# A decoder layer on one core: each modulation tile loaded and summed in one step, its sum queued behind the low part traced last

## The chip, the core and the metric

The kernel runs on one core of one Trainium2 chip. The metric is device time in microseconds (us) of one execution, and the median of several runs is compared. A profile is one execution recorded by the hardware profiler; its span goes from the first to the last instruction. The engines are TensorE (PE in the profile, its weight loads PEld), VectorE (DVE), ScalarE (ACT), GpSimd (POOL) and SyncE (SP), whose queue issues most transfers.

## The reference

One decoder layer over 256 tokens of width 2048, all in float32. A vector `c` gives six modulation vectors (shift, scale and gate for each of two sub-layers):

```python
mod = jax.nn.silu(c) @ w_ada[l] + b_ada[l]
sh1, sc1, g1, sh2, sc2, g2 = jnp.split(mod[:, None, :], 6, axis=-1)
h = x * (1.0 + sc1) + sh1
y = token_mixer(h, w_in[l], conv_w[l], a_log[l], dt_bias[l], gdn_norm_w[l], rel_bias,
                w_proj_moba[l], w_proj_gdn[l], w_out[l])
x = layer_norm(DEEPNORM_ALPHA * x + g1 * y, ln1_g[l], ln1_b[l])
h = x * (1.0 + sc2) + sh2
y = swiglu(h, w_ffn_in[l], w_ffn_out[l])
x = layer_norm(DEEPNORM_ALPHA * x + g2 * y, ln2_g[l], ln2_b[l])
```

The token mixer projects h to the inputs of a softmax attention (MoBA; with 256 tokens only its own causal block counts) and of a gated delta rule, runs both, projects and merges their outputs by sigmoid gates, and projects the sum. The modulation alone is a product of a 2048-vector with a 2048 x 12288 matrix: 100 MB that are read once and used for one multiplication per element.

## The kernel before

**Weights.** Every weight matrix is streamed in tiles of 128 partitions x 1024 float32 (0.5 MB). `step` lists one tile's work: `load_w` issues the transfer into `raw` on SP, `split_w` makes the rounded high part `hi` on ScalarE (L221) and the low part `lo = raw - hi` on VectorE (L222), and the matmuls take hi and lo three times over (L306 to L308 for 256 columns of tokens, L313 and L317 or L354 to L356 in the other layouts). One tile is 24 matmuls of 256 columns or their equal. `raw` is a ring of six buffers, `hi` and `lo` are rings of four each. `run(3)` writes the program down so that the loads and splits of up to four tiles ahead are traced before the matmuls of the current one.

**Modulation tiles.** The 12288 x 2048 matrix is laid out by output column, so that the product is a sum along the free axis: VectorE multiplies a tile by the broadcast silu(c) `cb` and adds up in one instruction (`ada_sum`, L241), and a short second instruction reads the accumulator. The first 40 columns come in the opening, in whole rows (tile `r`). The other 56 columns come later in two halves each, 112 tiles `raw_a` of 0.5 MB, which take their buffers from the same ring of six as the weights (L251). `ada_sums` is a generator: each advance issues one transfer and one sum. With its argument `ahead` at 1, the first advance issues two transfers, and every sum then belongs to the tile issued one advance earlier. Before each generator of 8 columns ends, its last tile is summed without a new load. The sum of the first half goes into `ada_half`, that of the second into `adac`.

**Pace.** `tick()` is called after the matmuls of every tile. It advances the lane "ada" 0.32 times a tick in the first part of the mixer, 0.85 times from the merge on, and 0.2 times in the second network; and it advances the background lanes with the small work of the two mixers: the convolutions (L581), the decay matrices (L685 to L701), the recursion that inverts the triangular blocks on VectorE (Mb, Ub, tm, L723 to L731), the block products (L754 to L818), the output norm (yb, L868) and the attention (L906 to L940).

**Order.** The kernel is written in a layer that schedules: instructions are taken by priority (in the main, the order in which they were traced) as soon as the layer's own timing model has their inputs ready. On each engine the resulting order is fixed, and the engine goes through it in that order; it waits at an instruction whose input is missing, and everything behind it waits too. `keep_in_program_order(i)` ties instruction i behind the one traced just before it on the same engine. It adds no wait on the chip, only an order. In the kernel before it is used for one low part of the second network, for some of the norm's operations and for a table load.

Of the kernel before, what the change touches and what calls it, by code (L numbers as in the profile page):

```python
# [13 lines left out]
OP = mybir.AluOpType  # L14
# [7 lines left out]
KT = D // P  # L22
# [71 lines left out]
def layer(ctx, tc, a, out):  # L94
    nc = tc.nc
    v_, s_, g_, t_, dma = nc.vector, nc.scalar, nc.gpsimd, nc.tensor, nc.sync
# [21 lines left out]
    cols = perm.tile([P, V_END], F32, name="cols")  # L118
# [8 lines left out]
    cb = perm.tile([P, D], F32, name="cb")  # L127
# [25 lines left out]
    adac = perm.tile([P, 96], F32, name="adac")  # L153
    w_ada = a["w_ada"]

    bg = {"moba": [], "main": [], "pre": [], "ada": []}
# [77 lines left out]

    ada_half = perm.tile([P, 64], F32, name="ada_half")

    def ada_sum(col, part, raw, parts):
        first, last = part == 0, part == parts - 1
        n = D // parts
        h = ada_half[:, col % 4:col % 4 + 1]  # L240
        v_.tensor_tensor_reduce(out=raw, in0=raw, in1=cb[:, n * part:n * part + n], scale=1.0,  # L241
                                scalar=cols[:, col:col + 1] if first else h, op0=OP.mult, op1=OP.add,
                                accum_out=adac[:, col:col + 1] if last else h)

    def ada_sums(order, ahead):
        todo = [(col, half) for col in order for half in range(2)]
        held = []
        for n in range(len(todo) + ahead):
            if n < len(todo):
                col, half = todo[n]  # L250
                raw = wp.tile([P, 1024], F32, tag="raw", name="raw_a", bufs=6)  # L251
                dma.dma_start(raw, w_ada.tile(8 * half, 8, col * P, P, by_column=True))
                held.append((col, half, raw))
            if n >= ahead:
                ada_sum(*held.pop(0), 2)
                yield 1.35

    def ada_opening(order, ahead, at_once, between):
# [61 lines left out]
    def pairs_of(ps):  # L320
        return ps.rearrange("p (t i) -> p t i", t=2)
# [91 lines left out]
    ada_order = [v * KT + j for k0, kn in GROUPS for j in range(k0, k0 + kn) for v in range(2)]  # L413
    ada_order += [v * KT + j for v in (2, 4, 3) for j in range(KT)]
    EARLY = 8
# [32 lines left out]
    def add_ba():  # L448
        wbs = [k1.tile([P, KT, 32], F32R, tag="c2", name=x, bufs=4) for x in ("wbh", "wbl")]
        split(*wbs, wba)  # L450
        ps = pg.tile([P, 512], F32, tag="gd", name="ps_ba")
        for f in range(KT):
            for w, h in ((0, 0), (0, 1), (1, 0)):
                t_.matmul(ps[:32, :S], wbs[w][:, f, :], h_ops[h][f], start=(f == 0 and w + h == 0),
                          stop=(f == KT - 1 and w == 1))
        s_.copy(ba, ps[:32, :S])
# [376 lines left out]
    def gdn_pre(b):  # L833
        yield from conv(kqs[b][:, 0:4, :], 4 * b)
        yield from conv(kqs[b][:, 4:8, :], 8 + 4 * b)
        yield from conv(vts[b], 16 + 8 * b)
        if b == 0:
            yield from until("begun")
            yield from zero_dram()
            make_sel()  # L840
        yield from gdn_qk(b)
        done.add(f"k{b}")
        yield from until("gates")
        yield from gdn_v(b)
        done.add(f"v{b}")
        pass

    def gdn_norm(b):
        yield from until(f"c{b}")
        o = bvs[b]  # L850
        on = c2("on", [P, 4, 2, 8])
        ss = on[:, 0]
        for h in range(8):
            for i in range(2):
                sq = c2("osq", [P, P])
                s_.activation(sq, o[:, i, h, :], AF.Square, accum_out=ss[:, i, h:h + 1])
            if h % 2 == 1:
                yield rest()
        v_.tensor_scalar(ss, ss, 1.0 / HD, None, op0=OP.mult)
        rs = on[:, 1]  # L860
        rsqrt(rs, on[:, 2], on[:, 3], ss, epsc[:, 0:1])
        yield 0.6
        yield from until(f"z{b}")
        yb = ybs[b]
        for h in range(8):
            for i in range(2):
                ys = yb[:, i, h * HD:(h + 1) * HD]
                v_.scalar_tensor_tensor(ys, o[:, i, h, :], rs[:, i, h:h + 1], ys, op0=OP.mult, op1=OP.mult)  # L868
            if h % 2 == 1:
                yield 1.1  # L870
        done.add(f"n{b}")

    def gdn_turn(b):
        yield from until(f"n{b}")
        yield rest()
        yb = ybs[b]
        if b == 0:
            hl = k1.tile([P, 2, 8, S], F32R, tag="ma0", name="ybA")
            hi, lo = hl[:, 0], [hl[:, 1, 0:4], hl[:, 1, 4:8]]
        else:  # L880
            hi = k1.tile([P, 8, S], F32R, tag="ma1", name="ybBh")
            lo = [k1.tile([P, 4, S], F32R, tag="m4", name="ybBl", bufs=3) for _ in range(2)]
        for f in range(8):
            ybT[0].append(hi[:, f, :])
            ybT[1].append(lo[f // 4][:, f % 4, :])
        for f in range(0, 8, 2):
            tp = pt.tile([P, 2, S], F32, tag="tp", name="tp")
            for i in range(2):
                for h in range(2):
                    t_.transpose(tp[:, i, h * P:(h + 1) * P], yb[:, h, (f + i) * P:(f + i + 1) * P], ident)  # L890
            split(hi[:, f:f + 2, :], lo[f // 4][:, f % 4:f % 4 + 2, :], tp, nwc)
            yield 0.6
            if f == 2:
                yield rest()
        done.add(f"t{b}")
# [49 lines left out]
    def begin():  # L945
        turn["all"] = True
        add_ba()
        ya = perm.tile([P, 2, MH, S], F32R, tag="s2", name="ya")
        for x in range(2):
            ya_ops[x].extend(ya[:, x, k, :] for k in range(MH))  # L950
        done.add("begun")
        pace.update(all=2.0, ada=0.32)
        bg["pre"] += [gdn_pre(1), gdn_norm(0)]
        bg["main"] += [gates_ba(), gdn_chain(0), gdn_chain(1), gdn_turn(0), gdn_norm(1), gdn_turn(1)]
        bg["moba"] += [moba(2), moba(3), moba(0), moba(1)]
        bg["ada"] += [ada_sums(ada_order[n:n + 8], 1) for n in range(2 * KT + EARLY, len(ada_order), 8)]

    do(begin)
    cur = {}

# [232 lines left out]
    def act(j, psg, psu):  # L1193
        ach, acl = cur["act"]
        sg = k3_tile("sg")
        s_.activation(sg, psg, AF.Silu)
        v_.tensor_tensor(sg, psu, sg, op=OP.mult)
        split(ach[:, 2 * j:2 * j + 2, :], acl[:, 2 * j:2 * j + 2, :], sg)
# [31 lines left out]
    begun, held = len(prog), []  # L1230
# [28 lines left out]
    def ffn_more():  # L1259
        act(0, pairs_of(pss[0]), pairs_of(pss[1]))  # L1260
        act(1, pairs_of(pss[2]), pairs_of(pss[3]))
        bg["main"].append(ln1_affine())
        bg["ada"].append(ada_sums(range(5 * KT, 6 * KT), 1))
        pace["ada"] = 0.2

    do(ffn_more)

    def ffn_unit(j):
# [115 lines left out]
```

## Time and profile before

| | us |
|---|---|
| median of 3 runs | 1711.68 |
| lowest and highest run | 1706.76 and 1713.21 |
| span of the profiled execution | 1708.3 |
| its TensorE busy | 1651.7 |
| its VectorE busy | 1235.5 |
| its ScalarE busy | 838.7 |

The profiled execution has no time of its own beside its span: the span is what the profiler gives, and the median of the runs lies 3.4 us above it. In the lines of the profile, an entry such as `[4.90 <-DVE lo L222]` says that the engine stood idle for 4.90 us before this instruction and that VectorE's `lo` at line 222 ended this. In the tables of waits the numbers are the total in us, how often, and the longest. In the tables of stretches each engine has its busy time and, in brackets, its instructions; the last three columns are the granted TensorE clock, the mean busy share of the 16 DMA engines, and GB/s. Line numbers are those of the kernel before; in the changed kernel everything from L245 on stands two lines lower.

### The profile page before, as it was taken

The numbers are of one execution on the slowest core, as the hardware profiler recorded it, in microseconds if no ns is written. First come the engines' busy times: TensorE is split into PE (matmuls) and PEld (weight loads), VectorE is DVE, ScalarE is ACT, GpSimd is POOL, SyncE is SP. The second block draws the span as 40 slices with busy tenths as digits, with TensorE's granted clock in tenths as the row PEclk, the third lists the DMA queues.
The fourth block names the chain that finished last, engine by engine and source line by source line (L and its number), as shares of the span: only waits on it lengthen the run. The fifth ranks groups of instructions, "written<-read, shape, count | busy, mean of one in ns | idle before, by whom it ended". The sixth has DMA issues, their size and how long they took to land.

```text
span 1708.3 us, 28200 instructions
## 1 busy us (share of the span) xinstructions
PE 1651.7 (97%) x11077; PEld 1482.3 (87%) x11077; DVE 1235.5 (72%) x1768; ACT 838.7 (49%) x1199; POOL 34.6 (2%) x60
## 2 busy tenths in 40 slices
PE   5899999999999998999999999999999999999997
PEld 4899999888999798889988998888888888888885
DVE  6899999787985676557989786666666666455454
ACT  3544445579653763364434454444444444433341
POOL 0000000010010000000000000000000000000000
PEclk9999999999999999999999999999999999999998
DMA  9999996666775577557899477777777776665661
GB/s 369 338 355 343 352 338 217 202 195 199 237 260 186 172 229 244 189 187 242 312 358 362 150 226 256 231 227 232 231 227 231 236 230 221 234 192 189 200 191 72
DMA packets 113750, 412.72 MB, mean 242 GB/s; under 512 B 13405, under 2 KB 14445, under 8 KB 108109
## 3 DMA queue, kind: packets, MB, share of 16 engines
q1 hardware_dynamic: 110178, 400.13, 69.4%
q0 software_dynamic: 3440, 10.80, 2.4%
q8 instruction: 87, 1.43, 0.3%
q14 instruction: 45, 0.37, 0.1%
HBM read 406.59 MB, written 4.28 MB: 241 GB/s over the span
## 4 chain that ended last, share of the span: by engine, by line
PE 61%; DVE 8%; DMA 5%; issue 2%; ACT 1%; DVEq 0%; ACTq 0%
PE mm L313 17%; PE mm L317 9%; PE mm L354 7%; PE mm L355 7%; PE mm L356 7%; DMA raw_a<-in_w_ada 4%; DVE lo L222 3%; PE mm L306 3%; PE mm L307 3%; PE mm L308 3%; DVE raw_a L241 1%; DMA Mb<-mbd 1%; PE ps L754 1%; DMA raw<-in_w_out 0%; ACT hi L221 0%
## 5 line engine op out<-in xcount | busy, mean ns | idle before, releaser
L221 ACT CAST hi<-raw 128x1024 fp32r<-128x1024 f32 (+2 forms) x576 | 582.6, 1015 | 706.2 <-PE mm L356 197.1
L222 DVE TENSOR_TENSOR lo<-raw,hi 128x1024 fp32r<-128x1024 f32 (+2 forms) x576 | 673.5, 1177 | 295.8 <-ACT hi L221 293.4
L306 PE MATMUL mm<-s,hi 128*128 128x256 f32 x1232 | 350.7, 285 | 15.9 <-ACT s L229 12.0
L308 PE MATMUL mm<-s,lo 128*128 128x256 f32 x1232 | 348.0, 283 | 13.1 <-DVE lo L222 12.9
L307 PE MATMUL mm<-s,hi 128*128 128x256 f32 x1232 | 346.8, 282 | 0.0
L313 PE MATMUL mm<-s,hi 128*128 128x512 f32 x1280 | 319.5, 392 | 0.0
L313 PEld LDWEIGHTS mm<-s,hi 128*128 128x128 f32 x1280 | 228.5, 188 | 39.4
L306 PEld LDWEIGHTS mm<-s,hi 128*128 128x128 f32 x1232 | 234.3, 190 | 21.0 <-ACT s L229 13.6
L308 PEld LDWEIGHTS mm<-s,lo 128*128 128x128 f32 x1232 | 235.8, 192 | 15.7 <-DVE lo L222 15.5
L307 PEld LDWEIGHTS mm<-s,hi 128*128 128x128 f32 x1232 | 234.8, 191 | 1.5 <-issue 1.1
L317 PEld LDWEIGHTS mm<-s,lo 128*128 128x128 f32 x1280 | 169.9, 188 | 13.6
L317 PE MATMUL mm<-s,lo 128*128 128x256 f32 x1280 | 171.9, 277 | 0.0
L354 PE MATMUL mm<-hi,ach 128*128 128x512 f32 x352 | 137.0, 389 | 0.0
L356 PE MATMUL mm<-hi,acl 128*128 128x512 f32 x352 | 136.9, 389 | 0.0
L355 PE MATMUL mm<-lo,ach 128*128 128x512 f32 x352 | 136.9, 389 | 0.0
L241 DVE CUSTOM_DVE_ANT_0 raw_a<-raw_a,cb,ada_half 128x1024 f32<-128x1024 f32 x56 | 71.7, 1280 | 53.3 <-DMA raw_a<-in_w_ada 53.3
L241 DVE CUSTOM_DVE_ANT_0 raw_a<-raw_a,cb,cols 128x1024 f32<-128x1024 f32 x56 | 71.8, 1281 | 51.1 <-DMA raw_a<-in_w_ada 51.0
L241 DVE CUSTOM_DVE_ANT_0 r<-r,cb,cols 128x2048 f32<-128x2048 f32 x40 | 93.4, 2346 | 9.4 <-ACT cb L137 9.4
L354 PE MATMUL mm<-hi,s 128*128 128x512 f32 x192 | 78.7, 410 | 0.0
L355 PEld LDWEIGHTS mm<-lo,ach 128*128 128x128 f32 x352 | 66.1, 188 | 13.8
L354 PEld LDWEIGHTS mm<-hi,ach 128*128 128x128 f32 x352 | 66.1, 188 | 13.8
L356 PEld LDWEIGHTS mm<-hi,acl 128*128 128x128 f32 x352 | 66.1, 188 | 13.6
(314 smaller groups left out, 2265.6 us busy)
## 6 DMA issues: line engine op xcount, KB each, us to landing
raw<-in_w_ffn_in SPq DMA_DIRECT2D x176, 512.0 KB, 4.3
raw<-in_w_in SPq DMA_DIRECT2D x160, 512.0 KB, 4.3
raw_a<-in_w_ada SPq DMA_DIRECT2D x112, 512.0 KB, 4.5
raw<-in_w_ffn_out SPq DMA_DIRECT2D x88, 512.0 KB, 4.2
r<-in_w_ada SPq DMA_DIRECT2D x40, 1024.0 KB, 8.0
raw<-in_w_in SPq DMA_DIRECT2D x48, 384.0 KB, 5.7
raw<-in_w_proj_gdn SPq DMA_DIRECT2D x32, 512.0 KB, 4.6
raw<-in_w_out SPq DMA_DIRECT2D x32, 512.0 KB, 5.9
```

The costliest lines, as they stand in the source:

```text
L221: s_.copy(hi, raw)
L222: low = v_.tensor_tensor(lo, raw, hi.bitcast(F32), op=OP.subtract)
L241: v_.tensor_tensor_reduce(out=raw, in0=raw, in1=cb[:, n * part:n * part + n], scale=1.0, scalar=cols[:, col:col + 1] if first else h, op0= ...
L306: t_.matmul(o, hi[:, i, c], ah, start=(first and i == 0 and t == 0), stop=False)
L307: t_.matmul(o, hi[:, i, c], al, start=False, stop=False)
L308: t_.matmul(o, lo[:, i, c], ah, start=False, stop=(last and i == kn - 1 and t == 1))
L313: t_.matmul(box[t].rearrange("p (u i) -> p u i", u=2), hi[:, i, t * P:(t + 1) * P], both[k0 + i], start=(first and i == 0), stop=False)
L317: t_.matmul(box[t][:, :S], lo[:, i, t * P:(t + 1) * P], both[k0 + i][:, 0, :], start=False, stop=(last and i == kn - 1))
L354: t_.matmul(box[h], xh, hi[:, i, :], start=start, stop=False)
L355: t_.matmul(box[h], xh, lo[:, i, :], start=False, stop=False)
L356: t_.matmul(box[h], xl, hi[:, i, :], start=False, stop=stop)
L754: t_.matmul(ps[to, n, :], lhs(n), rhs(n), start=True, stop=True)
```

## The change

Two things change, and both concern only the 112 tiles `raw_a`. `ahead` is 0 in all generators of `ada_sums`, so each advance issues a transfer and, in the same breath, the sum of that same tile. And the sum is tied behind the VectorE instruction traced last before it. Since the tiles of `run(3)` are traced ahead, this is in most cases the `lo` of a weight tile that will be used three or four tiles later. The opening (`ada_opening`) calls `ada_sum` without the tie and is as it was. The number of tiles, their bytes, the sums and the pace are the same.

```diff
-    def ada_sum(col, part, raw, parts):
+    def ada_sum(col, part, raw, parts, pin=False):
         first, last = part == 0, part == parts - 1
         n = D // parts
         h = ada_half[:, col % 4:col % 4 + 1]
-        v_.tensor_tensor_reduce(out=raw, in0=raw, in1=cb[:, n * part:n * part + n], scale=1.0,
-                                scalar=cols[:, col:col + 1] if first else h, op0=OP.mult, op1=OP.add,
-                                accum_out=adac[:, col:col + 1] if last else h)
+        added = v_.tensor_tensor_reduce(out=raw, in0=raw, in1=cb[:, n * part:n * part + n], scale=1.0,
+                                        scalar=cols[:, col:col + 1] if first else h, op0=OP.mult, op1=OP.add,
+                                        accum_out=adac[:, col:col + 1] if last else h)
+        if pin:
+            tc.keep_in_program_order(added)
...
             if n >= ahead:
-                ada_sum(*held.pop(0), 2)
+                ada_sum(*held.pop(0), 2, True)
                 yield 1.35
...
-        bg["ada"] += [ada_sums(ada_order[n:n + 8], 1) for n in range(2 * KT + EARLY, len(ada_order), 8)]
+        bg["ada"] += [ada_sums(ada_order[n:n + 8], 0) for n in range(2 * KT + EARLY, len(ada_order), 8)]
...
-        bg["ada"].append(ada_sums(range(5 * KT, 6 * KT), 1))
+        bg["ada"].append(ada_sums(range(5 * KT, 6 * KT), 0))
```

What it does to the order is seen at three places. The first is VectorE between the end of the second Ub recursion (about 663 us in the profile before) and the products that need z. Before, from the last step of the recursion on (lo: low part of a weight tile; raw_a: a sum, with ada_half or adac as its target and a short reading of the accumulator behind it):

```order
L222 TENSOR_TENSOR lo<-raw,hi 128x1024 x2
L241 ISA raw_a,ada_half<-raw_a,cb,cols 128x1024
L241 ISA ada_half 128x1
L222 TENSOR_TENSOR lo<-raw,hi 128x1024
L241 ISA raw_a,adac<-raw_a,cb,ada_half 128x1024
L241 ISA adac 128x1
L222 TENSOR_TENSOR lo<-raw,hi 128x1024 x2
L241 ISA raw_a,ada_half<-raw_a,cb,cols 128x1024
L241 ISA ada_half 128x1
L222 TENSOR_TENSOR lo<-raw,hi 128x1024 x3
L241 ISA raw_a,adac<-raw_a,cb,ada_half 128x1024
L241 ISA adac 128x1
```

The same place in the changed kernel:

```order
L222 TENSOR_TENSOR lo<-raw,hi 128x1024
L241 ISA raw_a,adac<-raw_a,cb,ada_half 128x1024
L241 ISA adac 128x1
L222 TENSOR_TENSOR lo<-raw,hi 128x1024 x4
L241 ISA raw_a,ada_half<-raw_a,cb,cols 128x1024
L241 ISA ada_half 128x1
L222 TENSOR_TENSOR lo<-raw,hi 128x1024 x3
L241 ISA raw_a,adac<-raw_a,cb,ada_half 128x1024
L241 ISA adac 128x1
```

Four sums became three, each sum now stands two to three tiles later in the count of sums than before, and the sums are spaced by three or four low parts. The second place is VectorE at the second Mb (L723), about 619 us in the profile before. Before:

```order
L723 SCALAR_TENSOR_TENSOR Mb<-Mb,bb 128x1024
L369 TENSOR_SCALAR on<-on 128x16
L729 TENSOR_TENSOR tm<-Ub,Mb 128x31
L370 TENSOR_TENSOR on<-on 128x16
L222 TENSOR_TENSOR lo<-raw,hi 128x1024
L868 SCALAR_TENSOR_TENSOR yb_6632<-v_92,on,yb_6632 128x128 x16
L222 TENSOR_TENSOR lo<-raw,hi 128x1024
L731 TENSOR_TENSOR Ub<-Ub,tm 128x31
L222 TENSOR_TENSOR lo<-raw,hi 128x1024
```

And in the changed kernel:

```order
L725 SCALAR_TENSOR_TENSOR Mb<-Mb,bb 128x1024
L371 TENSOR_SCALAR on<-on 128x16
L222 TENSOR_TENSOR lo<-raw,hi 128x1024
L372 TENSOR_TENSOR on<-on 128x16
L241 ISA raw_a,ada_half<-raw_a,cb,cols 128x1024
L241 ISA ada_half 128x1
L870 SCALAR_TENSOR_TENSOR yb_6630<-v_92,on,yb_6630 128x128 x16
L222 TENSOR_TENSOR lo<-raw,hi 128x1024
L731 TENSOR_TENSOR tm<-Ub,Mb 128x31
L222 TENSOR_TENSOR lo<-raw,hi 128x1024
```

A sum has moved in between the first low part behind Mb and the sixteen yb operations. The third place is SP, where the transfers are issued, around the first of these two places in time (raw: a weight tile). Before:

```order
L252 DMA raw_a<-in_w_ada 128x1024
L212 DMA raw<-in_w_in 128x1024 x7
L252 DMA raw_a<-in_w_ada 128x1024 x2
L212 DMA raw<-in_w_in 128x1024 x3
L252 DMA raw_a<-in_w_ada 128x1024
```

And in the changed kernel:

```order
L254 DMA raw_a<-in_w_ada 128x1024
L212 DMA raw<-in_w_in 128x1024 x3
L254 DMA raw_a<-in_w_ada 128x1024
L212 DMA raw<-in_w_in 128x1024 x4
L254 DMA raw_a<-in_w_ada 128x1024
```

At the change from one generator to the next, the two transfers in a row are gone: the modulation tiles are spread evenly among the weights.

## The prediction, made before the result was known

> **What bounds the kernel now.** I read the page first, then who TensorE waited for in the stretch in which modulation tiles are read beside small background work (300 to 1000 us), then the same for VectorE, then the stretches one by one.
>
> ```profile
> span 1708.3 us, 28200 instructions
> PE 1651.7 (97%) x11077; PEld 1482.3 (87%) x11077; DVE 1235.5 (72%) x1768; ACT 838.7 (49%) x1199; POOL 34.6 (2%) x60
> L222 DVE TENSOR_TENSOR lo<-raw,hi 128x1024 fp32r<-128x1024 f32 (+2 forms) x576 | 673.5, 1177 | 295.8 <-ACT hi L221 293.4
> L241 DVE CUSTOM_DVE_ANT_0 raw_a<-raw_a,cb,ada_half 128x1024 f32<-128x1024 f32 x56 | 71.7, 1280 | 53.3 <-DMA raw_a<-in_w_ada 53.3
> ```
>
> TensorE (PE) is busy for 1651.7 of 1708.3 us, so it is the bound, and 56.6 us of idle time is all that any change of order can win. VectorE (DVE) matters only where TensorE stands still for it.
>
> ```profile
> PE mm L308 <- DVE lo L222: 10.2, 6, 4.9
> PE mm L355 <- DVE lo L222: 2.1, 3, 1.3
> PE g L697 <- DVE ya L230: 1.7, 1, 1.7
> PE mm L307 <- DVE ya L230: 1.6, 1, 1.6
> PE rb L640 <- DVE pe L910: 1.0, 1, 1.0
> DVE raw_a L241 <- DMA raw_a<-in_w_ada: 64.4, 33, 8.4
> ```
>
> Between 300 and 1000 us TensorE waits 16.6 us for VectorE by these five rows. VectorE in turn stands 64.4 us, 33 times, in front of a sum whose tile has not landed. What hangs together is seen by laying VectorE's wait (in brackets, last column) beside the TensorE wait behind it:
>
> ```profile
> 358.86 1.28 DVE L241 CUSTOM_DVE_ANT_0 raw_a<-raw_a,cb,ada_half 128x1024 f32<-128x1024 f32 x1 [1.36 <-DMA raw_a<-in_w_ada]
> 360.74 0.50 PE L640 MATMUL rb<-gnr,sel 128*128 128x256 f32 x2 [1.01 <-DVE pe L910]
> 410.18 1.28 DVE L241 CUSTOM_DVE_ANT_0 raw_a<-raw_a,cb,ada_half 128x1024 f32<-128x1024 f32 x1 [2.12 <-DMA raw_a<-in_w_ada]
> 411.95 0.67 PE L697 MATMUL g<-kq 128*128 128x256 f32 x2 [1.70 <-DVE ya L230]
> 633.29 1.28 DVE L241 CUSTOM_DVE_ANT_0 raw_a<-raw_a,cb,ada_half 128x1024 f32<-128x1024 f32 x1 [1.10 <-DMA raw_a<-in_w_ada]
> 635.92 0.39 PE L308 MATMUL mm<-s,lo 128*128 128x256 f32 x1 [0.46 <-DVE lo L222]
> 648.16 1.28 DVE L241 CUSTOM_DVE_ANT_0 raw_a<-raw_a,cb,ada_half 128x1024 f32<-128x1024 f32 x1 [0.67 <-DMA raw_a<-in_w_ada]
> 650.85 0.39 PE L308 MATMUL mm<-s,lo 128*128 128x256 f32 x1 [1.04 <-DVE lo L222]
> 668.96 1.28 DVE L241 CUSTOM_DVE_ANT_0 raw_a<-raw_a,cb,cols 128x1024 f32<-128x1024 f32 x1 [3.69 <-DMA raw_a<-in_w_ada]
> 671.45 0.39 PE L308 MATMUL mm<-s,lo 128*128 128x256 f32 x1 [0.73 <-DVE lo L222]
> 683.30 1.28 DVE L241 CUSTOM_DVE_ANT_0 raw_a<-raw_a,cb,cols 128x1024 f32<-128x1024 f32 x1 [8.43 <-DMA raw_a<-in_w_ada]
> 685.79 0.58 PE L308 MATMUL mm<-s,lo 128*128 128x256 f32 x1 [4.90 <-DVE lo L222]
> 691.82 1.28 DVE L241 CUSTOM_DVE_ANT_0 raw_a<-raw_a,cb,ada_half 128x1024 f32<-128x1024 f32 x1 [3.82 <-DMA raw_a<-in_w_ada]
> 695.03 0.18 PE L778 MATMUL ps_a<-z,UU 32*32 32x32 f32 x1 [0.59 <-DVE z L773]
> 790.45 1.28 DVE L241 CUSTOM_DVE_ANT_0 raw_a<-raw_a,cb,cols 128x1024 f32<-128x1024 f32 x1 [3.09 <-DMA raw_a<-in_w_ada]
> 794.74 1.31 PE L890 MATMUL tp<-cst,yb 128*128 128x128 f32 x8 [0.47 <-DVE ybBl L233]
> 887.16 1.28 DVE L241 CUSTOM_DVE_ANT_0 raw_a<-raw_a,cb,ada_half 128x1024 f32<-128x1024 f32 x1 [2.88 <-DMA raw_a<-in_w_ada]
> 889.64 0.50 PE L355 MATMUL mm<-lo,mh 128*128 128x512 f32 x1 [1.34 <-DVE lo L222]
> ```
>
> So the sum is a stopper at the head of VectorE's queue, and the low parts behind it come late. The stall at 685.79 costs more than its 4.90 us, because the clock drops after it (seventh column):
>
> ```profile
> 672.00:681.00 9.00, 8.88 (x78) 8.68 (x76) 2.87 (x4) 2.59 (x3) 0.00 (x0) 1.00 1.00 350
> 681.00:690.00 9.00, 4.21 (x19) 4.21 (x20) 4.70 (x5) 1.80 (x3) 0.00 (x0) 0.67 0.57 192
> ```
>
> Granted clock 0.67 in the second stretch: 19 matmuls in 4.21 us are 0.222 us each, against 8.88/78 = 0.114 us before. 19 x 0.108 = 2.05 us.
>
> **Why the sums wait.** The raw ring has six buffers. A tile's transfer can be issued when the previous user of its buffer is done on VectorE, and takes this long (last row):
>
> ```profile
> L252 SPq DMA_DIRECT2D raw_a<-in_w_ada x112: 327/328/666, 306.9 to 1423.5; - x112
> DMA to landing us min/median/max: 3.3/4.5/9.4
> ```
>
> Following the buffers through both orders, I counted for each of the 112 tiles how many ring users stand on VectorE from the one that frees its buffer (or that of a load ahead of it on SP) to its own sum. Before it is 2 for 54 of them, and 1 to 7 overall: the sum has jumped the queue, and two users of 1.18 to 1.28 us are 2.5 us, less than the 4.5 us of a landing. In the changed order it is 6 for 93 and never under 5: five to six users are 6 to 7 us at least, and more where VectorE waits for TensorE. The weights give a little: 6 for 303 of 570 and up to 9 before, 6 for 548 now.
>
> **The change part by part.** Work is the same: 112 transfers, 112 sums, the same pace. Nothing but order and waits can move time.
>
> Removed: a TensorE wait can shrink by no more than VectorE's wait ahead of it. From the pairs between 300 and 800 us: 1.01 + 1.70 + 0.46 + 0.67 + 0.73 + 4.90 + 0.59 + 0.47 = 10.53 us. Of the three at 635 to 671 I count half, -0.93, since VectorE is nearly full there with the Ub recursion and a backlog may remain. The clock drop goes with the 4.90: 2.05 us. The one at 889.64 I count at nothing, because of this stretch:
>
> ```profile
> 650.00:700.00 50.00, 42.66 (x403) 41.11 (x404) 31.01 (x57) 17.81 (x26) 3.48 (x4) 0.93 0.72 237
> 800.00:950.00 150.00, 147.02 (x987) 133.69 (x986) 130.77 (x175) 60.85 (x63) 1.11 (x2) 1.00 0.91 329
> 1000.00:1450.00 450.00, 450.00 (x2661) 397.16 (x2660) 299.85 (x365) 219.36 (x287) 0.51 (x1) 1.00 0.73 234
> ```
>
> From 800 to 950 us the DMA engines are 0.91 busy, so a tile comes when the transfers allow it, wherever its sum stands; bounds 0 and 1.34. From 1000 us on TensorE never stops (450.00 of 450.00), although VectorE's sums wait there too: the 32 sums of the second network are worth 0, covered by 150 us of idle VectorE time.
>
> Added: at the second Mb wait the new order puts one sum between that wait and the 16 yb operations, ahead of two low parts (second place shown with the change).
>
> ```profile
> 618.94 1.23 DVE L723 SCALAR_TENSOR_TENSOR Mb<-Mb,bb 128x1024 f32<-128x1024 f32 x1 [4.50 <-issue]
> 621.54 4.28 DVE L868 SCALAR_TENSOR_TENSOR yb<-v,on,yb 128x128 f32<-128x128 f32 x16
> 627.01 0.39 PE L308 MATMUL mm<-s,lo 128*128 128x256 f32 x1 [2.24 <-DVE lo L222]
> ```
>
> The TensorE wait of 2.24 us at 627.01 then grows by that sum: 1.28 us. Bounds: 0 if a lighter VectorE reaches the place with more low parts done (it stood idle 4.50 us for Mb, so not likely), and 1.28 plus a clock drop. One stall of 4.90 us brought the drop, this one of 2.24 us did not; 3.5 us lies between, nearer to the one without, and I take none. The Trainium skill ("TensorE: Matmul & The Clock Gate", part 1) has the clock halve after an idle window of about 3.4 us that runs freely; by it 3.5 us may be enough, which costs some 2 us more in the sum, and the 0.67 above agrees with it.
>
> Sum: 10.53 - 0.93 + 2.05 - 1.28 = 10.4 us less. Against the profiled execution that is 1708.3 - 10.4 = 1697.9 us of span; the runs' median of 1711.68 lies 3.4 us above that span, so **1701.3 us**.
>
> **Rivals.** (1) Hidden anyway: what stands behind a sum today then stands behind the next thing, the Mb wait, 16 yb operations, or a hi part whose transfer is late at 672 to 681 us, where the DMA engines are 1.00 busy. For it: only 16.6 us of TensorE waits face 64.4 us of VectorE waits, and the largest (4.90) falls into that transfer crowd. Then half of the 4.90 and its clock drop remain, 3.5 us, and half of the other small ones: a gain of 4 to 5 us, 1707. (2) The sum waits where it now stands. Load and sum in one step leave no tile in hand, and from 800 to 950 us every second ring user is such a tile:
>
> ```profile
> 800.00:950.00 150.00, 42.78 (x34) 1.00 0.91 329
> ```
>
> If each of these 34 sums waited out one tile's transfer (0.524 MB at 329 GB/s, 1.6 us), that is 54 us on VectorE, whose idle time there is 150 - 130.77 = 19.2 us; 35 us would reach TensorE, less the 10 won earlier: 1737. It turns the sign from (19.2 + 10.4) / 34 = 0.9 us a sum. Against it: the 5 to 6 ring users ahead. The Trainium skill ("Trainium Kernel Development and Optimization", best practices) asks for double buffering so that transfers overlap with compute, which speaks for this rival; no row of before shows the new place. (3) The change does not do what it says, because the tie holds VectorE's order only and lets a load slip behind; the loads on SP stand one by one in the new order, so I give it little: no change, 1711.
>
> **How the numbers follow.** My forecast 0.60, rival 1 0.26, rival 2 0.08, rival 3 0.06. About 0.5% (8.6 us, below 1703.1 or above 1720.2) is what a measurement of this kernel tells from no change. The forecast falls below 1703.1 in nine tenths of its weight, rival 1 in a tenth: faster 0.56; slower is rival 2 and a little: 0.09; the rest, 0.35, within. Lower end: all 16.6 us and the clock go, 18.7 less, 1693. Upper end: rivals 1 and 3 and the runs' own highest, 1713. Rival 2 is left out of the range.
>
> **What would show it.** Right: VectorE's wait for raw_a between 300 and 1000 us falls from 64.4 us to under 20; TensorE's wait on lo at L308 from 10.2 to under 6; clock 1.00 from 650 to 700 us; the wait behind yb near 627 us longer than 2.24. Wrong: the raw_a waits are gone and TensorE's are not (rival 1), or raw_a waits grow between 800 and 950 us and TensorE's lo waits with them (rival 2).

## The result and the profile after

| | before | changed |
|---|---|---|
| median of 6 runs each, us | 1712.77 | 1697.70 |
| lowest and highest, us | 1706.76 and 1714.14 | 1691.40 and 1699.48 |
| span of the profiled execution, us | 1708.3 | 1694.9 |

The ratio is 0.9914, with a 95% interval of 0.9898 to 0.9929. The forecast was 1701.3 us, with a range of 1693 to 1713. The sign and the stage were right. The profiled execution is 13.4 us shorter, where the sum had said 10.4.

The head of the page of the changed kernel, and one of its groups of instructions:

```profile
span 1694.9 us, 28166 instructions
PE 1646.1 (97%) x11077; PEld 1478.7 (87%) x11077; DVE 1236.2 (73%) x1768; ACT 839.8 (50%) x1199; POOL 34.6 (2%) x60
L222 DVE TENSOR_TENSOR lo<-raw,hi 128x1024 fp32r<-128x1024 f32 (+2 forms) x576 | 675.5, 1178 | 365.4 <-ACT hi L221 362.6
```

VectorE does the same work in the same time (1236.2 against 1235.5 us). TensorE stands idle for 1694.9 - 1646.1 = 48.8 us, where it was 56.6; and its busy time is 5.6 us shorter although it does the same 11077 matmuls. So only part of the gain is waiting; the rest is matmuls that ran faster, and a section below takes the two apart.

Who TensorE waits for between 300 and 1000 us, then the first two rows of the same view for VectorE:

```profile
PE mm L310 <- DVE lo L222: 4.1, 2, 3.5
PE tpn L1181 <- DVE r L1173: 2.5, 4, 2.0
PE mm L357 <- DVE lo L222: 0.3, 1, 0.3
DVE lo L222 <- ACT hi L221: 96.2, 72, 5.6
DVE z L790 <- PE ps L756: 9.6, 4, 2.8
```

The row of 64.4 us in front of `raw_a` is gone, and none has come back in this stretch. VectorE now waits for high parts instead, 96.2 us where it was 64.4. That costs little: by the first and the third row TensorE waits 4.4 us for a low part in this stretch. TensorE's wait for a low part of 256 columns (L308, now L310) fell from 10.2 to 4.1 us, and 3.5 of these are one stall. The stretches:

```profile
600.00:650.00 50.00, 45.89 (x387) 45.49 (x386) 40.69 (x94) 26.07 (x44) 2.25 (x3) 0.97 0.76 243
650.00:700.00 50.00, 50.00 (x508) 48.72 (x507) 33.15 (x58) 21.22 (x31) 3.49 (x4) 1.00 0.79 259
800.00:950.00 150.00, 147.18 (x959) 134.15 (x958) 131.64 (x187) 60.33 (x64) 1.11 (x2) 1.00 0.88 323
1000.00:1450.00 450.00, 450.00 (x2608) 394.87 (x2607) 296.36 (x360) 217.27 (x285) 1.48 (x3) 1.00 0.74 233
```

From 650 to 700 us TensorE is busy without a break at full clock, with 508 matmuls where there were 403. In the stretch before, the clock shows 0.97: this is the price of the second Mb. VectorE there:

```profile
615.59 1.23 DVE L725 SCALAR_TENSOR_TENSOR Mb<-Mb,bb 128x1024 f32<-128x1024 f32 x1 [4.56 <-issue]
616.81 1.22 DVE L222 TENSOR_TENSOR lo<-raw,hi 128x1024 fp32r<-128x1024 f32 x1
618.03 1.28 DVE L241 CUSTOM_DVE_ANT_0 raw_a<-raw_a,cb,cols 128x1024 f32<-128x1024 f32 x1
619.23 4.28 DVE L870 SCALAR_TENSOR_TENSOR yb<-v,on,yb 128x128 f32<-128x128 f32 x16
623.43 1.22 DVE L222 TENSOR_TENSOR lo<-raw,hi 128x1024 fp32r<-128x1024 f32 x1
624.71 0.39 PE L310 MATMUL mm<-s,lo 128*128 128x256 f32 x1 [3.54 <-DVE lo L222]
625.90:629.20 3.30, 3.30 (x18) 3.30 (x18) 3.30 (x7) 0.63 (x1) 0.00 (x0) 0.50 0.84 269
```

The sum stands between the low part and the sixteen yb operations, as the order had shown. TensorE waits 3.54 us where it waited 2.24, and then its clock is 0.50 for 3.3 us (last row, a stretch of the same kernel).

Laid beside each other by the time at which the k-th high part of each kernel starts, the changed one is 3.9 us ahead at 307 us of the kernel before, 4.4 at 569, 1.5 at 647 (the Mb stall), 13.0 at 738, 15.6 at 890, and 13.1 from 1031 us to the end. So some 11 us are won between 647 and 738 us, nothing in the second network, and 3.9 us at a place where the change has not yet touched anything: its first tile is loaded at 303 us.

### The profile page after: what moved, and what is told of

The parts are those of the page before. It is cut to its first block, busy times and chain, and to the rows that moved or that the text cites. A ratio compares the mean times of both kernels' runs of the same rounds, so it can differ in the third digit from the quotient of the medians.

```text
span 1694.9 us, 28166 instructions
## 1 busy us (share of the span) xinstructions
PE 1646.1 (97%) x11077; PEld 1478.7 (87%) x11077; DVE 1236.2 (73%) x1768; ACT 839.8 (50%) x1199; POOL 34.6 (2%) x60
## 4 chain that ended last, share of the span: by engine, by line
PE 62%; DVE 7%; DMA 4%; ACT 3%; issue 2%; POOL 0%; DVEq 0%; ACTq 0%; POOLq 0%
PE mm L315 17%; PE mm L319 9%; PE mm L356 7%; PE mm L358 7%; PE mm L357 7%; PE mm L308 4%; PE mm L309 4%; PE mm L310 3%; DVE lo L222 3%; DMA raw<-in_w_out 1%; DVE raw_a L241 1%; ACT hi L221 1%; DMA raw<-in_w_proj_gdn 1%; PE ps L756 1%; DMA UU<-ubd 0%
## 5 line engine op out<-in xcount | busy, mean ns | idle before, releaser
L308 PE MATMUL mm<-s,hi 128*128 128x256 f32 x1232 | 349.0, 284 | 16.1 <-ACT s L229 12.0
L310 PE MATMUL mm<-s,lo 128*128 128x256 f32 x1232 | 345.2, 281 | 8.1 <-DVE lo L222 7.9
L308 PEld LDWEIGHTS mm<-s,hi 128*128 128x128 f32 x1232 | 234.1, 190 | 21.3 <-ACT s L229 13.6
L310 PEld LDWEIGHTS mm<-s,lo 128*128 128x128 f32 x1232 | 234.1, 190 | 10.0 <-DVE lo L222 9.9
L356 PE MATMUL mm<-hi,s 128*128 128x512 f32 x192 | 78.2, 407 | 0.0
L358 PE MATMUL mm<-hi,s 128*128 128x512 f32 x192 | 77.0, 401 | 0.0
L357 PE MATMUL mm<-lo,s 128*128 128x512 f32 x192 | 76.1, 396 | 0.0
```

The costliest lines, as they stand in the source:

```text
L308: t_.matmul(o, hi[:, i, c], ah, start=(first and i == 0 and t == 0), stop=False)
L310: t_.matmul(o, lo[:, i, c], ah, start=False, stop=(last and i == kn - 1 and t == 1))
L356: t_.matmul(box[h], xh, hi[:, i, :], start=start, stop=False)
L357: t_.matmul(box[h], xh, lo[:, i, :], start=False, stop=False)
L358: t_.matmul(box[h], xl, hi[:, i, :], start=False, stop=stop)
```

## The experiments

**The kernel before, once more,** as a measure of what one profile is worth. No edit.

> The kernel before, unchanged, profiled once more. It asks two things. First, are the raw_a waits and the stalls behind them the same in every execution? If the stall of 4.90 us at 685.79 and the clock drop behind it belong to the order of the instructions, they are here again within 0.5 us; if they were an accident of one execution (a transfer that happened to take 9.4 us), TensorE's longest wait between 300 and 1000 us is well under 4 us here. Second, the two profiles differ by 3.7 us already before 300 us, where their instructions stand in the same order: if this is scatter between executions, it moves again here (opening shorter by up to 4 us); if not, the opening is as in the first profile of the kernel before. Time: 1708 to 1714, ratio 1.000 within 0.002.

Measured: 1712.9 us, ratio 0.9986 (0.9963 to 1.001). The span is 1713.9 us, 5.6 above the first profile of the same kernel.

```profile
PE mm L308 <- DVE lo L222: 10.2, 6, 4.1
DVE raw_a L241 <- DMA raw_a<-in_w_ada: 68.5, 33, 7.7
650.00:700.00 50.00, 42.99 (x392) 41.92 (x393) 31.57 (x60) 17.09 (x25) 3.48 (x4) 0.90 0.72 238
```

The waits return at the same places with nearly the same sums; the stall of 4.90 us is 4.1 here, a little outside the 0.5 us that I had allowed. Up to 307 us this execution is 2.1 us faster than the first, so part of the lead there is scatter. What differs most is the clock: here it halves four times between 410 and 704 us, in the first profile once. The first time is behind a stall of 2.03 us, with the clock in the 3.4 us behind it:

```profile
410.18 1.11 PE L697 MATMUL g<-kq 128*128 128x256 f32 x2 [2.03 <-DVE ya L230]
410.30:413.70 3.40, 3.40 (x15) 3.22 (x16) 3.20 (x6) 1.09 (x2) 0.00 (x0) 0.50 0.81 198
```

The waits belong to the program; whether a clock drop follows one is different from execution to execution.

**Load and sum in one step, without the tie.** Against the changed kernel:

```diff
-                ada_sum(*held.pop(0), 2, True)
+                ada_sum(*held.pop(0), 2)
```

> The change without the tie: each tile is loaded and summed in one step (no tile in hand), but the scheduler may again place the sum where it likes. My theory (what counts is how many ring users stand between the one that frees a tile's buffer and the tile's sum): the order has 2 for 60 of the 112 tiles and 1 to 6 overall, as before, so the raw_a waits stay, 50 us or more between 300 and 1000 us, and the time is that of before: 1705 to 1715. Rival (what counts is that no buffer of the ring is held by a waiting modulation tile, so that weights run deeper): most of the gain is here, 1698 to 1703, and the raw_a waits shrink to under 30 us.

Measured: 1723.82 us, ratio 1.0055 (1.0028 to 1.0083): slower than before, and above what I had expected.

```profile
PE mm L310 <- DVE lo L222: 12.4, 8, 4.6
DVE raw_a L241 <- DMA raw_a<-in_w_ada: 71.2, 40, 9.2
800.00:950.00 150.00, 143.99 (x945) 128.47 (x944) 131.40 (x174) 60.27 (x64) 1.10 (x2) 1.00 0.92 323
```

Without the tie the scheduling layer puts the sums where its own timing model thinks the tile has landed: 2 ring users ahead for 60 of the 112, and 1 to 6 overall, much as before, but now without a tile in hand. TensorE stands idle for 65.3 us in all, against 56.6 to 59.9 in three profiles of the kernel before. Taking that tile away is therefore no gain in itself. The tie is what moves the sums back. Why the time rises by some 9 us I did not follow up.

**The tie alone, with one tile still in hand.** Against the changed kernel:

```diff
-        bg["ada"] += [ada_sums(ada_order[n:n + 8], 0) for n in range(2 * KT + EARLY, len(ada_order), 8)]
+        bg["ada"] += [ada_sums(ada_order[n:n + 8], 1) for n in range(2 * KT + EARLY, len(ada_order), 8)]
...
-        bg["ada"].append(ada_sums(range(5 * KT, 6 * KT), 0))
+        bg["ada"].append(ada_sums(range(5 * KT, 6 * KT), 1))
```

> The tie alone: a tile is still summed one advance after its load (one tile in hand), and the sum is tied behind the low part traced last. The order has 5 to 13 ring users ahead of each sum (9 for most), and 4 to 6 ahead of a weight tile in place of 6 and more. My theory: raw_a waits between 300 and 1000 us nearly gone (under 5 us), as in the changed kernel, and most of the gain; the weights have one ring user less ahead, which at 1.2 us each costs something only where the transfers are crowded (800 to 950 us, and 672 to 681 us): 1697 to 1705. Rival (the gain is the freed buffer): no gain or a loss, 1708 to 1720, with waits of hi for its transfer in place of those of the sums.

Measured: 1712.02 us, ratio 0.9989 (0.9967 to 1.0011). This was a miss: no gain, though no sum waits at all.

```profile
ACT hi L221 <- DMA raw<-in_w_out: 42.0, 22, 6.3
ACT hi L221 <- DMA raw<-in_w_proj_gdn: 35.1, 14, 4.0
650.00:700.00 50.00, 49.99 (x500) 49.01 (x499) 35.21 (x64) 21.68 (x30) 3.48 (x4) 1.00 0.81 265
800.00:950.00 150.00, 140.52 (x887) 124.58 (x886) 125.09 (x166) 55.90 (x58) 1.10 (x2) 0.99 0.90 315
```

The stretch 650 to 700 us is as good as in the changed kernel, and at 738 us this kernel is 7 us ahead of before. Then it loses 15 us up to 1053 us. A tile in hand plus a late sum keeps a buffer for 5 to 13 ring users (9 for 39 tiles), and the weights have what is left: 4 users for 20 of them, 5 for 303, 6 for 247. ScalarE waits for the transfers of `w_proj_gdn` and `w_out` (35.1 and 42.0 us; 7.2 and 23.5 before; in the changed kernel the two rows below), and TensorE is busy for 140.5 of 150 us instead of 147. The two halves of the change need each other: the tie makes the sums late enough, and giving up the tile in hand pays the buffer for it.

```profile
ACT hi L221 <- DMA raw<-in_w_out: 38.3, 23, 4.0
ACT hi L221 <- DMA raw<-in_w_proj_gdn: 14.7, 9, 2.7
```

**The change in the second network only** (`ahead` 0 and the tie for its 32 sums, the kernel before elsewhere). Against the kernel before, without the lines of the tie:

```diff
-        bg["ada"].append(ada_sums(range(5 * KT, 6 * KT), 1))
+        bg["ada"].append(ada_sums(range(5 * KT, 6 * KT), 0))
```

> The change in the 32 tiles of the second network alone; the 80 tiles of the mixer are loaded and summed as before. My theory: from 1000 us on TensorE never stops in either profile, so this is worth nothing: 1708 to 1714, although the raw_a waits after 1000 us (39.9 us before) fall to under 3 us. Rival (VectorE's waits slow TensorE in a way that the idle time does not show, through late low parts at the head of each unit): a gain in proportion to the waits removed, 39.9 of 104 us, 5 us or more: under 1707.

Measured: 1713.17 us, ratio 1.0000 (0.9977 to 1.0022). The wait of 39.9 us for `raw_a` behind 1000 us is gone, and the time has not moved, as the term of zero said.

**The changed kernel, once more.** No edit.

> The changed kernel once more, on the same chip and beside the same runs of before as the three that follow. It is the measure for them, and a second profile of the same order. In the first profile the stall at the second Mb was 3.5 us and a clock drop of 3.4 us followed it; and 3.7 us of the shorter span were won before 300 us, where both kernels have the same order. My theory: the ratio to before is 0.990 to 0.994 again; raw_a waits between 300 and 1000 us are none; the stretch 650 to 700 us has TensorE busy 49.9 us or more. If the gain before 300 us is scatter of the chip and not of the kernel, the opening here is as long as that of before (the 122nd hi part at 304.6 us or later), and the span is 2 to 4 us longer than 1694.9 with the same ratio.

Measured: 1697.24 us, ratio 0.9921 (0.9897 to 0.9944), span 1696.2. The Mb stall is there again (3.2 us; the clock halves at 622 us for 6.8). If the lead ahead of 307 us were scatter, I had written, the opening would be as long here as before; the lead was there again, 3.7 us. That did not refute scatter, as the third execution of the kernel before showed later (below).

**The Mb step asked for two calls of its lane later,** in the changed kernel, so that VectorE does not stand in front of it.

```diff
-        yield rest(6)
+        yield rest(8)
```

> The changed kernel with the start of the Ub recursion put off by two more ticks (the pause before the Mb operation 8 in place of 6), so that Mb's transfer has landed when VectorE gets there. In the order the 16 yb operations and two sums then stand ahead of the second Mb. My theory of the term that the change adds: the stall of 3.5 us at the second Mb and the clock drop behind it go, 3.5 + 1.7 us, while the recursion ends some 5 us later, which nothing waits for: 1690 to 1695, 3 to 6 us under the changed kernel in this job. Rival (the recursion is on the path: what follows it is paced by it): the stall goes and comes back as a wait on the products behind the recursion, no gain within 2 us.

Measured: 1695.66 us, ratio 0.9905 (0.9883 to 0.9928); not to be told from the changed kernel's 0.9914 and 0.9921.

```profile
600.00:650.00 50.00, 50.00 (x425) 49.85 (x425) 45.59 (x105) 28.12 (x49) 2.24 (x3) 1.00 0.78 249
700.00:800.00 100.00, 97.82 (x767) 87.72 (x766) 66.06 (x102) 52.86 (x99) 0.00 (x0) 1.00 0.63 204
PE mm L357 <- DVE lo L222: 2.4, 4, 0.8
PE mm L308 <- ACT ybA L232: 1.3, 1, 1.3
```

TensorE no longer stops between 600 and 650 us and the clock stays at 1.00. At 647 us this execution is 8.5 us ahead of before, the changed kernel 1.5; 2 us of the difference of 7 are from the opening. (Between 690 and 790 us the small matmuls stand at other places of the order, and the k-th high part is no measure there.) By 818 us the difference is 4.2: between 700 and 800 us TensorE, now earlier, is busy for 97.82 us where it was for 99.98, and waits for ybA and for low parts that it found ready in the changed kernel. At the end 1.5 us are left, no more than the opening brought. The stall is gone, and waits that it had covered have come out in its place: the rival had the time right, and only the place wrong.

**The change in the third group of eight columns only** (its 16 tiles are summed between about 670 and 810 us). Against the kernel before:

```diff
-        bg["ada"] += [ada_sums(ada_order[n:n + 8], 1) for n in range(2 * KT + EARLY, len(ada_order), 8)]
+        bg["ada"] += [ada_sums(ada_order[n:n + 8], int(n != 2 * KT + EARLY + 16), n == 2 * KT + EARLY + 16) for n in range(2 * KT + EARLY, len(ada_order), 8)]
```

(The last argument says whether the sums are tied.)

> The change in the third group of eight columns alone, that is the 16 tiles summed from about 660 to 800 us; the other 96 tiles are as before. In the order the second Mb has no sum behind it, as in the kernel before. My theory: the largest term, the stall of 4.90 us at 685.79 with its clock drop, and the small ones at 671, 695 and 794 us go with this group alone, 7 to 9 us; the stall of 2.24 us at the second Mb stays as it was: 1703 to 1706, ratio 0.995 within 0.002, with TensorE busy over 49.5 us from 650 to 700 us. Rival (the tie helps by its share of sums, or the crowd of transfers at 672 to 681 us brings the stall anyway): a gain of 2 us or less, 1710 or more.

Measured: 1701.28 us, ratio 0.9938 (0.9917 to 0.996).

```profile
DVE raw_a L241 <- DMA raw_a<-in_w_ada: 19.9, 14, 3.7
650.00:700.00 50.00, 48.94 (x496) 47.49 (x495) 35.23 (x62) 20.77 (x30) 3.48 (x4) 1.00 0.78 256
```

16 of 112 tiles bring about 70% of the change (10.5 of some 15 us of median), more than the 7 to 9 us expected. Between 647 and 707 us this kernel wins 9.7 us on the one before. The pairs of waits of this group in that stretch (0.73 + 4.90 + 0.59 us) and the clock's 2.05 make 8.3.

**A ring of five buffers** in the changed kernel, to see whether it is depth that the tie alone was short of.

```diff
-        raw = wp.tile([P, 1024], F32, tag="raw", name="raw", bufs=6)
+        raw = wp.tile([P, 1024], F32, tag="raw", name="raw", bufs=5)
...
-                raw = wp.tile([P, 1024], F32, tag="raw", name="raw_a", bufs=6)
+                raw = wp.tile([P, 1024], F32, tag="raw", name="raw_a", bufs=5)
```

> The changed kernel with a raw ring of five buffers in place of six, so that weights and sums have 5 ring users ahead of them in place of 6. The tie alone (with one tile in hand) left the weights 4 to 5 and lost all of its gain between 770 and 1000 us, where hi waited for its transfers. If the reason is the depth that is left to the weights, this kernel shows the same loss at the same place: hi's waits for the tiles of w_proj_gdn and w_out between 300 and 1000 us 60 us or more (changed kernel 53, tie alone 77), 4 to 12 us over the changed kernel, and no raw_a waits before 800 us. If the loss of the tie alone had another reason (sums that come late in themselves, since they stand 9 users behind), this kernel is within 2 us of the changed one.

Measured: 1711.27 us, ratio 1.0011 (0.9992 to 1.0031).

```profile
ACT hi L221 <- DMA raw<-in_w_out: 40.8, 22, 6.2
ACT hi L221 <- DMA raw<-in_w_proj_gdn: 31.8, 14, 3.6
800.00:950.00 150.00, 141.80 (x901) 126.61 (x900) 126.41 (x167) 56.60 (x58) 1.10 (x2) 0.99 0.90 315
```

One buffer less costs what the tile in hand cost: the same two waits on ScalarE, the same stretch, the same 141 of 150 us. The sums hardly wait here either (0.6 us in two). So the loss of the tie alone is the weights' lost depth, shown in two ways. It is 14 us behind the changed kernel measured beside it, where I had expected 4 to 12. A ring of seven was not tried.

**Breaking up equal matmuls.** In both kernels, before and changed, one matmul of 256 columns in every third tile is done as two of 128. The reason lies in the section after this one: the lead ahead of 307 us is a matter of how far apart matmuls start.

```diff
-                t_.matmul(o, hi[:, i, c], al, start=False, stop=False)
+                if i == 1 and t == 0 and broken[0] % 3 == 0:
+                    t_.matmul(o[:, :P], hi[:, i, c], al[:, :P], start=False, stop=False)
+                    t_.matmul(o[:, P:], hi[:, i, c], al[:, P:], start=False, stop=False)
+                else:
+                    t_.matmul(o, hi[:, i, c], al, start=False, stop=False)
```

> The kernel before, and in every third tile of the 256-column layout (L300) one matmul of 256 columns is done as two of 128; the modulation tiles are as before. Both traces of the kernel before show 1204 to 1247 matmuls of 256 columns in one piece between 168 and 308 us, all 117.8 ns apart; the changed kernel has the same matmuls there 113.3 ns apart, and nothing else differs in that stretch. Theory A (the spacing is picked anew at each interruption of equal matmuls, and then stays): the piece falls into some 16 pieces of 70, some at 113.3 and some at 117.8 ns, and the stretch 200 to 300 us holds 875 to 895 matmuls instead of 856 in 100 us. Theory B (the spacing belongs to the place in the program: its buffers, its addresses, its transfers): 117.8 ns in all pieces, 850 to 858 matmuls. Time: some 100 more matmuls of at most 0.06 us each are up to 6 us by both; A takes 2 to 5 us back: 1710 to 1720.

> The changed kernel with the same split of one matmul in every third tile. Theory A: the piece from 168 to 308 us, 1247 matmuls all 113.3 ns apart in two traces, becomes a mixture of both spacings, 865 to 885 matmuls in 200 to 300 us instead of 889. Theory B: 113.3 ns in all pieces, about 885 with the split ones. Time: by A 1698 to 1708, by B 1697 to 1703. The waits for raw_a stay under 5 us by both.

Measured: 1722.89 us for the kernel before with breaks, ratio 1.0067 (1.0043 to 1.0092), and 1698.72 us for the changed one, ratio 0.9927 (0.9903 to 0.9951). The first is above the expected 1710 to 1720. The two stretches from 200 to 300 us, in this order:

```profile
200.00:300.00 100.00, 100.00 (x883) 100.00 (x883) 95.86 (x133) 52.91 (x70) 3.11 (x5) 1.00 0.75 268
200.00:300.00 100.00, 100.00 (x883) 100.00 (x883) 96.14 (x132) 53.11 (x71) 3.11 (x5) 1.00 0.74 266
```

For the kernel before neither theory had it; for the changed one B did. The pieces between two breaks are not mixed: from 168 to 308 us all of them run at about 113.5 ns per matmul, in both kernels. A break costs 0.113 us more than the matmul it replaces (the three starts around it lie 57, 113 and 170 ns apart, 340 ns in place of 227), and there are 82 of them, 9.3 us. Against the mean of three executions of the kernel before, in the terms of the table below, the kernel before with breaks pays 9.3 us for the breaks, gets 6.2 of the long spacing back, and has 3.4 us more idle time and 4.7 us more at half clock: 11.2 us, where its span is 11.1 longer. Why it stands idle more I did not follow up.

**The kernel before, a third time.** No edit.

> The kernel before, unchanged, a third time. If the spacing of the 256-column matmuls between 168 and 308 us is picked by chance at the wait ahead of it, this execution may show 113.3 ns where two showed 117.8; if it belongs to the program, 117.8 again. The waits for raw_a between 300 and 1000 us 60 to 72 us, the stall of TensorE behind one of them 4 to 5.5 us near 686 us.

Measured: 1713.6 us, ratio 1.0015 (0.9985 to 1.0044), span 1712.0. The waits are the same (68.2 us for `raw_a`, 5.6 us the longest of TensorE behind a low part). But from 168 to 308 us this execution has the short spacing, and it leads the first by 4.8 us at 307 us. It is then overtaken: the clock halves four times between 432 and 896 us.

**Both small wins together:** the changed kernel with `rest(8)` and with the break in every twelfth tile only.

```diff
-        yield rest(6)
+        yield rest(8)
...
+                if i == 1 and t == 0 and broken[0] % 12 == 0:
```

> The changed kernel with the second Mb asked for two calls of its lane later (rest(8) for rest(6)), and with one matmul of 256 columns split into two of 128 in every 12th tile of the 256-column layout (L300). The split ended every piece of matmuls at 117.8 ns where it was tried in every third tile, and costs 0.113 us each. Here about 21 splits cost 2.4 us and can save the 117.8 ns pieces of more than one or two tiles, which held 5.8 us in the changed kernel with the later Mb: the sum of the slow spacing falls to under 3.5 us. Theory: the splits are worth 0 to 2 us net, the stall at Mb stays away, 1692 to 1697 us, a ratio of 0.988 to 0.992. Rival: the two make no difference beyond the changed kernel, 1696 to 1700 us, because what is won ahead of 300 us and at Mb is given back in front of VectorE between 770 and 1000 us.

Measured: 1696.42 us, ratio 0.9895 (0.9881 to 0.9909), five runs between 1695.80 and 1697.85. It has the lowest ratio of the study, but its interval overlaps those of the changed kernel and of the later Mb, and theory and rival both allow its time. TensorE's idle time is 50.1 us, the clock costs it 5.8 us, the long spacing 3.1.

## Two spacings of the same matmul

This I had not expected, and it is behind most of the 3.9 us ahead of 307 us. Between 168 and 308 us TensorE does 1200 to 1250 matmuls of 256 columns without a pause, the same ones in all kernels here but those with breaks. The stretch 200 to 300 us in the first and the third execution of the kernel before, then in the changed kernel:

```profile
200.00:300.00 100.00, 100.00 (x851) 100.00 (x850) 95.69 (x126) 49.19 (x64) 2.57 (x4) 1.00 0.81 284
200.00:300.00 100.00, 100.00 (x885) 100.00 (x884) 97.69 (x130) 51.30 (x69) 3.11 (x5) 1.00 0.82 284
200.00:300.00 100.00, 100.00 (x885) 100.00 (x884) 97.90 (x131) 51.39 (x67) 3.12 (x5) 1.00 0.81 286
```

TensorE is 100.00 of 100 us busy at clock 1.00 in all three, and does 851 matmuls in one and 885 in the others. The starts lie either 113.3 or 117.8 ns apart, and a piece keeps to one of the two, but for the end of this one. In the first execution 1247 matmuls in a row (168.1 to 315.0 us) have a mean of 117.6. The last 48 of these have weights of 32 columns (L454) in place of 128, and the last 32 alone are at 113.3. In the changed kernel the same 1247 (167.3 to 308.9 us) have 113.3. 1247 x 4.3 ns is 5.4 us. A piece keeps the spacing that it has after its start: of some 240 unbroken pieces of 48 matmuls or more in eleven executions, all but six have one spacing throughout, and the six are this piece with its last 32. Between two pieces lies an interruption, in this stretch mostly a wait of 0.1 to 1 us. Of those eleven executions six ran this piece at 117.8 and five at 113.3, and the kernel before shows both, so neither spacing belongs to one program alone. Whether the change makes the short one likelier is open: the four executions with both of its halves for all 112 tiles ran at 113.3, and six of the seven others at 117.8. A long piece of equal matmuls multiplies whatever is settled at its start; matmuls of another width inside it ended the long spacing in this piece in all three kernels that had them. At 307 us the five with the short spacing are 2.1 to 5.9 us ahead of the first profile, the six with the long one 0 to 2.1. Why there are two is not settled here.

With this, the difference of the spans can be taken apart. Idle is the span less TensorE's busy time. Clock is half of TensorE's busy time at half clock, counted from 50 us on. Spacing is the excess over 113.3 ns in all unbroken pieces whose mean lies between 116.8 and 119 ns; how short a piece is counted moves these figures by some tenths, the last row by 0.2.

| execution | span | idle | clock | spacing |
|---|---|---|---|---|
| before | 1708.3 | 56.6 | 5.1 | 9.2 |
| before, again | 1713.9 | 57.4 | 11.0 | 10.4 |
| before, third | 1712.0 | 59.9 | 12.8 | 4.6 |
| changed | 1694.9 | 48.8 | 4.0 | 6.1 |
| changed, again | 1696.2 | 47.8 | 7.2 | 5.8 |
| mean of three less mean of two | 15.9 | 9.7 | 4.0 | 2.1 |

The three columns add up to 15.8 of 15.9 us. Idle time is steady from execution to execution; the clock and the spacing are not.

## Why the prediction was right, and where it was off

**The mechanism held.** The sums no longer wait (64.4 us to none, under 20 was asked for), TensorE's wait for low parts at that line fell to 4.1 us (under 6), the clock from 650 to 700 us is 1.00, and the stall behind yb is longer than 2.24 us. All four signs named in advance came, and the third group alone won 9.7 us where its pairs of waits and the clock add up to 8.3. One sentence ahead of the sum was wrong: that 56.6 us of idle time are all that a change of order can win. TensorE's busy time fell by 5.6 us too.

**Removed waits, 10.53 - 0.93 us.** With the Mb stall of 1.28 against them the sum had idle time fall by 8.3 us. It fell by 7.8 in the first pair of profiles and by 9.7 over all five. In the first pair alone, idle time and clock (5.1 to 4.0 us) give 8.9 us, less than the forecast 10.4; that the span fell by 13.4 there is the spacing's 3.1, and 1.4 that stand in none of the three. The discount of 0.93 for a backlog from 635 to 671 us was not needed: no wait of that size is left there. The stall at 889.64 us, counted at nothing, went too (the L355 row fell from 2.1 to 0.3 us); in its place four waits at L1181 grew from 0.9 to 2.5 us, so the zero was right in the sum and wrong in its reason, that tiles come there when the transfers allow it.

**The clock, 2.05 us, is the term that was too small.** It was read from one execution that had one drop between 50 and 1600 us, and up to 690.0 us only, where the drop lasts to 690.9. Over three executions the stalls of the kernel before cost 9.6 us in clock, 7.1 without the last few matmuls of the program, which lose 2.3 to 2.5 us in every kernel; in the changed kernel it is 5.6 and 3.2. The change is worth 4.0 us here.

**Mb, 1.28 us: the stall was sized right (2.24 to 3.54 us) and its clock drop, which I took as none, came** in both executions of the changed kernel. 18 matmuls in 3.30 us at clock 0.50 lose 1.65 us. In fourteen executions the clock halved 38 times between 50 and 1600 us, each time for 3.4 or 6.8 us, and 29 of these drops came behind stalls shorter than 3.4 us, among them 2.03 us in the row above. The same Mb stall of 2.24 us that brought no drop in the first profile brought one in the kernel with only the second network changed, at 634.5 us, and no stall of more than 2.61 us stayed without one.

The traces also show what decides it. Within one execution all the drops begin whole multiples of 3.413 us apart: in the second execution of the kernel before at 410.3, 652.6, 686.8 and 697.0 us, which is 71, 10 and 3 steps of that length. Lay each span out in these steps, and take those between 50 and 1600 us that begin at full clock: all 35 in which TensorE was idle for 1.84 us or more were followed by a drop, 3 of 14 with 1.44 to 1.84 us, and none of the other 5678. So what counts is how much of a stall falls into one step. My estimate from these figures is that a stall of 2.24 us, lying anywhere, stays under 1.84 us in both steps that it touches four times in ten, and one of 3.5 us once in twenty. By this, a stall that grows to 3.5 us should have been priced with the drop, 1.65 us more.

The rule of the Trainium skill that I had set against my choice ("TensorE: Matmul & The Clock Gate", part 1: half clock after an idle window of about 3.4 us that runs freely) gave the right answer here. The traces agree with the length of its window and with its running freely; they do not agree if the whole window has to be idle, since 1.84 us of it were always enough.

**The second network, 0.** Confirmed by the change made there alone (ratio 1.0000, 0.9977 to 1.0022).

**Rival 1** (hidden anyway) was right about one thing only: the time that the later Mb saved was largely covered. **Rival 2** (the sum waits where it now stands) did not happen: from 800 to 950 us no sum waits, and TensorE is busy 147.18 of 150 us as before. But its mechanism sits close by. With a tile in hand, or with a ring of five, the waits come back on the weights and TensorE loses 5 to 7 us in that stretch, and about 10 from 770 to 1000 us. I had followed the ring users ahead of the sums and said of the weights only that they "give a little"; the step from 6 users to 5 for half of them is worth the whole change. **Rival 3** fell with the first row.

**What the sum left out:** the two spacings, 3.1 us of the first pair's difference. One profile of the kernel before could not show that there are two, and that the changed kernel met the short one in front of 309 us was luck, as far as the forecast goes.

## What to carry to other kernels

In a ring that two kinds of work share, count for each user how many others stand between the one that frees its buffer and its own turn: with 4.5 us from issue to landing and 1.2 us a user, two were too few for the sums here, and five or six were enough. For the weights five in place of six were too few where the transfers are crowded, and cost as much as the whole change brings: every extra buffer that one kind holds is taken from the other. A wait on an engine that is not the bound is priced by laying it beside the bound's wait behind it, and the clock that such a stall costs by more than one execution, since it depends on where the stall happens to lie. Before a gain of a few microseconds is put down to a change, look whether it arises where the change is; here 3.9 of the 13.4 us between the first two profiles stood in a stretch that the change had not reached.
